# Product steps between the scan's operations: two in a row at every other place

## The chip, the cores and the metric

The kernel runs on one core of a Trainium2 chip. The metric is the device time of one execution in microseconds (us), smaller is better. The core's engines are TensorE (PE in the profile; PEld is its weight load), VectorE (DVE), ScalarE (ACT), GpSimd (POOL) and SyncE (SP), which here only issues DMAs.

## What is computed

The program is a trunk of two layers over 512 latent tokens (and 256 context tokens) of width 1024. Each layer is a token mixer and a mixture of experts:

```
for layer in range(DEPTH):                      # DEPTH = 2
    ...
    bg, cg, ha, rw, ga, gb = split(h_lat @ w_in)            # one wide input product
    ya = (bg * conv(cg * ha)) @ w_a_out                     # branch A: gated convolution
    # branch B: RWKV-7, a scan over tokens, forward and backward, for 8 heads of 64
    s = s * w_t - (s . kk_t) b_t + v_t k_t ;  y_t = s . r_t
    yb = readout(y) @ w_b_out
    y_lat = (sigmoid(ga) * ya + sigmoid(gb) * yb) @ w_o
    ...
    x = x + g2 * hier_moe(h)                                # 32 experts, top 2
```

In layer 0 the context tokens are carried through as well (768 tokens in the products), in layer 1 only the latent ones leave the layer (512 tokens in the products that concern us).

## The kernel before

A layer runs through four stages: `stage_dense` (the columns of `w_in` that the scan needs, and its preparation), `stage_scan`, `stage_out` (`w_b_out`, `w_o`, the router) and `moe` (the experts' weights stream through three rings of buffers, `er`, `ez` and `ex`).

The change is in `stage_scan`. The scan is worked in chunks of 64 tokens, 12 chunks (`NCK`) in each of two passes (`a` = 0, 1, four heads each). The work on a chunk is a chain of small matmuls with copies between them on ACT and DVE:

- `chunk()` prepares the next chunk: transposes L898 (ACT copies L899 and L900), transposes L907 of the keys (ACT copy L909 into `KTr`).
- `step()` is one chunk of the scan: L937 and L941 into `pc`; ACT copies that to `W` (L944); L951 multiplies `W` with the inverse `Rf`; a DVE copy (L952) and an ACT copy (L953) bring the two halves to `VU`; L960 makes the state's update (added on DVE, L964); L975 and L977 make the outputs `Y`.
- `inverses()` makes, for six chunks (`H`) at a time, the triangular inverses `Rf` that those chunks need. It begins with the products L823, then ACT copies L829, a DVE transpose L834, a chain of 31 pairs of DVE operations (L842, L844), two long DVE transposes (L846 into `dgRc`, L848 into `AlTc`), and ends with rounds of L866, ACT copies L870 (`Yb`), L876 and ACT copies L879 on PE and ACT. Each layer makes four such chains; while DVE works at the three later ones, the steps of the six chunks before them run on PE.
- `readout()` normalises the finished outputs: L1000, DVE L1002, ACT L1004, L1008, a row of small DVE operations ending in L304 (`yr`), L1013, and DVE L1015 to L1020.

These chains leave PE idle while a copy runs. So the scan also carries the layer's other products: `fillers()` is a generator over the rest of `w_in` (the convolution's columns, the gates) and the first products of `w_a_out`. One **step** of it (one `next`) is one slice of 128 rows of a product: the three kinds `hh,wh`, `hl,wh` and `hh,wl` of L333, for two column segments in layer 0 (six matmuls) and one in layer 1 (three). Every fourth step begins with the load of a weight tile, which ACT (L314, `wh`) and DVE (L315, `wl`) split into two parts. Before some products stands additional work of the modulation (L653, L252 on PE). The first products of `w_a_out` read `ah` and `al` in place of `hh` and `hl`.

Every `yield w` in `step()`, `chunk()`, `inverses()` and `readout()` is a **place**, where `run()` calls `fill(w)`: it adds `w * FILL[l]` to a debt `owed`, and does a step for each whole unit of it:

```
FILL = (0.75, 0.75)
...
            owed[0] += w * FILL[l]
            while owed[0] >= 1.0:
                owed[0] -= 1.0
                if not held:
                    if next(filler, None):
                        held.append(True)
```

The weights `w` are 1 or 2 in `step()` and `chunk()`, so a place gets none, one or two steps. `held` is set when the products of `w_a_out` reach the point (`HOLD`) from which they are kept for the scan's end.

PE's instructions stand in the order in which the code is written (`tc.manual_schedule` for PE). The orders of DVE, ACT, POOL and SP are made by a scheduler, which has PE's order to go by; they change when the steps move.

Of the kernel before, what the change touches and what calls it, by code (L numbers as in the profile page):

```python
# [116 lines left out]
class Trunk:  # L117
# [606 lines left out]
    def stage_scan(self):  # L724
        nc, tc, t, l = self.nc, self.tc, self.t, self.l
        fp = self.fp
        self.sp = tc.alloc_tile_pool(name=f"sp{l}", bufs=1, side=self.B, reuse_waits="tile")
        self.St = {}
        self.Yt = {}
        filler = self.filler  # L730
        owed = [0.0]
        held = []
        aux = []

        def fill(w):
            if aux:
                aux[0][1] -= 1
                if aux[0][1] < 0:
                    n = next(aux[0][0], None)
                    if n is None:  # L740
                        aux.pop(0)
                    else:
                        aux[0][1] = n
            owed[0] += w * FILL[l]
            while owed[0] >= 1.0:
                owed[0] -= 1.0
                if not held:
                    if next(filler, None):
                        held.append(True)

        def run(gen, pause=False):


            for w in gen:
                if w < 0 and pause:
                    return
                fill(w if w >= 0 else -w - 1)
        with tc.manual_schedule(engines={mybir.EngineType.PE}):
            bs = [(a, g) for a in range(2) for g in range(NCK // H)]
            fill(FIRST[l])  # L760
            inv = self.inverses(*bs[0])
            run(inv)
            cur = self.inv
            nxt = self.chunk(0, 0)
            run(nxt)
            for n, (a, g) in enumerate(bs):
                inv = self.inverses(*bs[n + 1]) if n + 1 < len(bs) else iter(())
                for ii in range(H):
                    i = g * H + ii
                    if ii in RUN[l]:  # L770
                        run(inv, True)
                    mine = self.ch
                    if (n, ii) != (len(bs) - 1, H - 1):
                        nxt = self.chunk(*((a, i + 1) if i + 1 < NCK else (a + 1, 0)))
                    else:
                        nxt = iter(())
                    run(self.step(a, i, *cur, *mine, nxt))
                    for c in SETS:
                        if i == (CCK - 1 if c[1] < CCK else c[1]) and c[0] >= self.c0:
                            aux.append([self.readout(a, c), 0])  # L780
                run(inv)
                cur = self.inv
            held.clear()
            while aux:
                fill(TAIL / FILL[l])
            for _ in filler:
                pass
        self.oa.release()
        self.sp.release()
        fp.release()  # L790
# [784 lines left out]
```

## Time and profile before

| | |
|---|---|
| median of 3 runs | 2934.89 us (2927.92 to 2936.92) |
| the profiled execution | 2937.82 us, span 2935.9 us, mean granted TensorE clock 0.92 |
| PE | 2526.1 us busy, 86% of the span, 17809 matmuls |
| DVE | 1237.9 us, 42% |
| ACT | 837.2 us, 29% |
| POOL | 451.2 us, 15% |
| DMA | mean 251 GB/s |

The share of a whole span is an average over stages with different limits, so the stages are read one by one. The scan of layer 0 lies between about 280 and 824 us of the span, that of layer 1 between about 1793 and 2245 us; the experts of layer 0 run from about 1000 us, those of layer 1 from about 2370 us. The granted clock is given as a share of full speed: 1.00 is 2.4 GHz, 0.50 is 1.2 GHz, a value between is a stretch with some of each. An entry "[0.69 <-ACT KTr L909]" at a row's end is the engine's idle time just before the instruction, and what ended it.

### The profile page before, as it was taken

To read this page: it belongs to the slowest core of one execution; us is meant where nothing else is said; L and a number is where in the kernel's file an instruction comes from. 1 tells how busy PE (TensorE), PEld (TensorE's weight loads), DVE (VectorE), ACT (ScalarE), POOL (GpSimd) and SP (SyncE) were. 2 spreads that over 40 slices of the span, in tenths; PEclk is the share of its full clock that TensorE was granted. 3 is DMA by queue.
4 is the path that set the end of the run, shared out by engine and by line. 5 is a ranking of instruction groups with operands and counts; after the bars stand their busy time and mean duration, and the time that the engine had idled before them with its cause. 6 is when DMAs were issued, how large, how long until landed. Compare 5 with 4: busy or idle time off the path is not lost. (4 is left out here: it accounts for less than half of the span.)

```text
span 2935.9 us, 44964 instructions
## 1 busy us (share of the span) xinstructions
PE 2526.1 (86%) x17809; PEld 1657.8 (56%) x17809; DVE 1237.9 (42%) x2626; ACT 837.2 (29%) x1603; POOL 451.2 (15%) x558
## 2 busy tenths in 40 slices
PE   7898898998889697979796998788988869888896
PEld 5676676777678443434246775566766734333334
DVE  4486654636453411111115686566546421111113
ACT  4453333333222111111112453333442211111111
POOL 0132011111130201111102132011211021111101
PEclk9899999999999798989897999889989979899998
DMA  7657454553553899999984377554445589999993
GB/s 290 211 158 221 169 166 163 180 186 101 173 195 140 324 408 391 391 360 394 383 324 139 110 193 243 180 176 160 153 126 181 221 333 405 408 403 386 400 391 107
DMA packets 287141, 737.21 MB, mean 251 GB/s; under 512 B 57168, under 2 KB 144464, under 8 KB 230864
## 3 DMA queue, kind: packets, MB, share of 16 engines
q1 hardware_dynamic: 273648, 702.83, 66.0%
q0 software_dynamic: 13280, 31.48, 3.3%
q8 instruction: 141, 2.31, 0.3%
q14 instruction: 72, 0.59, 0.1%
HBM read 647.44 MB, written 99.88 MB: 255 GB/s over the span
## 5 line engine op out<-in xcount | busy, mean ns | idle before, releaser
L333 PE MATMUL pd<-hh,wh 128*128 128x512 f32 (+1 forms) x912 | 352.1, 426 | 14.0 <-ACT wh L314 7.9
L333 PE MATMUL pd<-hh,wl 128*128 128x512 f32 (+1 forms) x912 | 311.6, 382 | 11.0 <-DVE wl L315 11.0
L333 PE MATMUL pd<-hl,wh 128*128 128x512 f32 (+1 forms) x912 | 310.6, 381 | 1.3 <-DVE hl L315 1.1
L1413 PE MATMUL pd<-ez,xs 128*64 128x512 f32 x1024 | 255.8, 619 | 42.7 <-DMA ez<-in_w 42.0
L315 DVE TENSOR_TENSOR wl<-wr,wh 128x512 fp32r<-128x512 f32 x236 | 166.0, 704 | 235.4 <-ACT wh L314 234.2
L314 ACT ACTIVATE wh<-wr 128x512 fp32r<-128x512 f32 x236 | 148.5, 630 | 323.1 <-PE pd L333 214.0
L1434 DVE TENSOR_TENSOR yo<-py,yo 64x1024 f32<-64x1024 f32 x65 | 79.0, 1215 | 337.3 <-ACT yo L1433 324.2
L333 PEld LDWEIGHTS pd<-hh,wh 128*128 128x128 f32 x912 | 163.0, 197 | 94.6 <-issue 29.5
L1422 DVE COPY hs<-pd 128x512 f32<-128x512 f32 x65 | 44.9, 690 | 351.1 <-PE pd L1413 312.6
L333 PEld LDWEIGHTS pd<-hh,wl 128*128 128x128 f32 x912 | 163.4, 197 | 47.2 <-DVE wl L315 14.8
L333 PEld LDWEIGHTS pd<-hl,wh 128*128 128x128 f32 x912 | 164.4, 198 | 29.8 <-DVE hl L315 2.6
L1413 PE MATMUL pd<-er,xs 128*64 128x512 f32 x672 | 177.2, 624 | 0.8 <-DMA er<-in_w 0.8
L1413 PEld LDWEIGHTS pd<-ez,xs 128*64 128x64 f32 x1024 | 77.5, 141 | 174.0 <-issue 124.7
L1426 PEld LDWEIGHTS pt<-cst,hs 128*128 128x128 f32 x1040 | 128.7, 197 | 82.1 <-issue 46.2
L1426 PE MATMUL pt<-cst,hs 128*128 128x64 f32 x1040 | 143.3, 287 | 19.0 <-DVE hid L1429 10.7
L1388 POOL DMA_INDIRECT xe<-h2rows,slot x64 | 60.9, 951 | 635.8 <-PE px L1401 616.9
L1413 PE MATMUL pd<-ex,xs 128*64 128x512 f32 x384 | 111.6, 666 | 30.8 <-DMA ex<-in_w 30.8
L1413 PE MATMUL py<-ez,hid 128*64 128x512 f32 x520 | 127.8, 616 | 11.7 <-DVE yo L1434 8.9
L1429 DVE TENSOR_TENSOR hid<-hid,pt 128x256 f32<-128x256 f32 x65 | 27.2, 418 | 234.5 <-ACT hid L1428 233.8
L1424 ACT ACTIVATE hs<-pd 128x512 f32<-128x512 f32 x65 | 38.8, 597 | 288.0 <-PE pd L1413 244.0
L1403 ACT ACTIVATE xs<-px 128x512 f32<-128x512 f32 x65 | 38.7, 597 | 276.7 <-PE pd L1413 142.7
L1433 ACT ACTIVATE yo<-py 64x1024 f32<-64x1024 f32 x65 | 66.4, 1021 | 179.6 <-PE py L1413 152.3
(382 smaller groups left out, 4536.9 us busy)
## 6 DMA issues: line engine op xcount, KB each, us to landing
ez<-in_w SPq DMA_DIRECT2D x193, 1024.0 KB, 16.8
er<-in_w SPq DMA_DIRECT2D x125, 1024.0 KB, 15.4
ex<-in_w SPq DMA_DIRECT2D x72, 1024.0 KB, 13.1
wm<-in_w_mod SPq DMA_DIRECT2D x48, 1024.0 KB, 6.5
wr<-in_w_in SPq DMA_DIRECT2D x172, 256.0 KB, 3.1
bufY<-zrow SPq DMA_DIRECT2D x28, 512.0 KB, 6.8
dKB<-KB SPq DMA_DIRECT2D x16, 768.0 KB, 5.4
dRR<-RR SPq DMA_DIRECT2D x16, 768.0 KB, 4.8
```

Of the source, the lines that this page charges most:

```text
L314: self.nc.scalar.activation(hi, src, AF.Copy)
L315: self.nc.vector.tensor_tensor(lo, src, hi, op=ALU.subtract)
L333: nc.tensor.matmul(p, a[:, k], h[:, kt, s], start=kt == 0 and j == 0, stop=kt == nk - 1 and j == 2)
L1388: self.nc.gpsimd.indirect_dma_start(out=xe[:], out_offset=None, in_=self.h2[:], in_offset=bass.IndirectOffsetOnAxis(ap=slot, axis=0), boun ...
L1403: nc.scalar.activation(xs, ps, AF.Copy)
L1413: nc.tensor.matmul(out[h * CAP:(h + 1) * CAP, c:c + 512], a[:, kt, :], w[:, i + h, c:c + 512], start=kt < 2, stop=kt >= nk - 2)
L1422: nc.vector.tensor_copy(hs, ps)
L1424: nc.scalar.activation(hs, ps, AF.Copy)
L1426: nc.tensor.matmul(pt[:, i, c, :], hs[:, c * P:(c + 1) * P], k["ii"], start=True, stop=True)
L1429: nc.vector.tensor_tensor(hid, hid, pt[:, 1], op=ALU.mult)
L1433: nc.scalar.activation(yo, py[CAP:], AF.Copy)
L1434: nc.vector.tensor_tensor(yo, py[:CAP], yo, op=ALU.add)
```

## The change

The debt is now paid in pairs: `fill()` waits until it is two, and then does two steps at the same place.

```
             owed[0] += w * FILL[l]
-            while owed[0] >= 1.0:
-                owed[0] -= 1.0
-                if not held:
-                    if next(filler, None):
+            while owed[0] >= 2.0:
+                owed[0] -= 2.0
+                for _ in range(2):
+                    if not held and next(filler, None):
                         held.append(True)
```

The steps are the same and as many; PE has as many instructions as before, and its scan operations stand in the same order. What moves are the steps between them. Counted in PE's order, the places that have any step go from 156 to 107 in layer 0 and from 149 to 105 in layer 1, and no place is more than one step ahead or behind of where it was.

On PE, in layer 1, a chunk of the scan after L951 (`pc<-W,Rf`), to the next chunk's transposes. Before:

```order
L951 MATMUL pc<-W,Rf 64x64 x8
L333 MATMUL pd<-hh,wh 128x512
L333 MATMUL pd<-hl,wh 128x512
L333 MATMUL pd<-hh,wl 128x512
L960 MATMUL pc<-VU,KTr 64x64 x8
L333 MATMUL pd<-hh,wh 128x512
L333 MATMUL pd<-hl,wh 128x512
L333 MATMUL pd<-hh,wl 128x512
L898 MATMUL pA<-cst,vfb 128x128 x2
L333 MATMUL pd<-hh,wh 128x512
L333 MATMUL pd<-hl,wh 128x512
L333 MATMUL pd<-hh,wl 128x512
```

The same place on PE after the change:

```order
L951 MATMUL pc<-W,Rf 64x64 x8
L960 MATMUL pc<-VU,KTr 64x64 x8
L333 MATMUL pd<-hh,wh 128x512
L333 MATMUL pd<-hl,wh 128x512
L333 MATMUL pd<-hh,wl 128x512
L333 MATMUL pd<-hh,wh 128x512
L333 MATMUL pd<-hl,wh 128x512
L333 MATMUL pd<-hh,wl 128x512
L898 MATMUL pA<-cst,vfb 128x128 x2
L907 MATMUL py<-cst,KBs 128x128 x4
```

One step each stood before L960, before L898 and before L907; now L960 follows L951 directly, two steps stand before L898, and L907 follows L898 directly.

On DVE, in layer 0, the end of the third of the four inversion chains (the last of its L842 and L844, then the two long transposes), with the `VU` copy L952 of the step that runs beside it. Before:

```order
L842 TENSOR_TENSOR tmp<-AlTc,Tl 128x31
L303 SCALAR_TENSOR_TENSOR yg<-yz,yg 128x4
L844 TENSOR_TENSOR Tl<-Tl,tmp 128x31
L315 TENSOR_TENSOR wl<-wr,wh 128x512
L300 TENSOR_TENSOR yz<-yg 128x4
L846 STREAM_TRANSPOSE dgRc<-Tl 128x32x32
L848 STREAM_TRANSPOSE AlTc<-Tl 128x32x32
L952 COPY VU<-pc 64x256
L301 SCALAR_TENSOR_TENSOR yz<-yz,yv 128x4
```

The same end on DVE after the change:

```order
L842 TENSOR_TENSOR tmp<-AlTc,Tl 128x60
L952 COPY VU<-pc 64x256
L300 TENSOR_TENSOR yz<-yg 128x4
L844 TENSOR_TENSOR Tl<-Tl,tmp 128x2x30
L268 TENSOR_TENSOR mod_83<-pd,pv_82 128x8
L301 SCALAR_TENSOR_TENSOR yz<-yz,yv 128x4
L842 TENSOR_TENSOR tmp<-AlTc,Tl 128x31
L272 SCALAR_TENSOR_TENSOR am_84<-mod_83,pv_82 128x8
L304 SCALAR_TENSOR_TENSOR yr<-yz,yg 128x256
L844 TENSOR_TENSOR Tl<-Tl,tmp 128x31
L846 STREAM_TRANSPOSE dgRc<-Tl 128x32x32
L848 STREAM_TRANSPOSE AlTc<-Tl 128x32x32
```

The `VU` copy and a readout's last operation (`yr`, L304) stood behind the two transposes and now stand ahead of them.

On DVE, in layer 1, the second inversion chain: the place of its last `VU` copy, before:

```order
L842 TENSOR_TENSOR tmp<-AlTc,Tl 128x175
L952 COPY VU<-pc 64x256
L844 TENSOR_TENSOR Tl<-Tl,tmp 128x7x25
L842 TENSOR_TENSOR tmp<-AlTc,Tl 128x156
L844 TENSOR_TENSOR Tl<-Tl,tmp 128x6x26
L842 TENSOR_TENSOR tmp<-AlTc,Tl 128x135
```

That copy after the change:

```order
L842 TENSOR_TENSOR tmp<-AlTc,Tl 128x31
L844 TENSOR_TENSOR Tl<-Tl,tmp 128x31
L846 STREAM_TRANSPOSE dgRc<-Tl 128x32x32
L848 STREAM_TRANSPOSE AlTc<-Tl 128x32x32
L952 COPY VU<-pc 64x256
L315 TENSOR_TENSOR wl<-wr,wh 128x512
L964 TENSOR_TENSOR St_14909<-pc,S_15678 64x4x64 x2
L656 TENSOR_TENSOR mrow<-mrow,pd 128x512
```

It stood seven pairs of the chain ahead of the chain's end; it now stands behind the chain's end and both transposes.

## Rows read from the trace of the kernel before

**Rows 1.** Windows of whole stages: us, busy of each engine, PEclk, DMA share, GB/s.

```profile
280.00:824.00 544.00, 486.57 (x5149) 386.16 (x5150) 291.18 (x743) 183.45 (x419) 73.49 (x126) 0.95 0.51 166
1000.00:1530.00 530.00, 462.23 (x2316) 198.91 (x2314) 78.50 (x120) 80.61 (x126) 55.09 (x60) 0.92 0.98 383
...
1793.00:2245.00 452.00, 378.37 (x4068) 277.84 (x4066) 267.69 (x638) 169.23 (x380) 73.92 (x128) 0.91 0.53 172
```

**Rows 2.** PE's waits, layer 0's scan: us in total, times, longest us.

```profile
PE pA L866 <- DVE AlTc L848: 13.5, 2, 10.7
PE pA L1013 <- DVE yr L304: 12.6, 7, 3.7
PE pd L333 <- ACT ah L314: 6.0, 1, 6.0
PE pc L951 <- ACT W L944: 4.4, 4, 1.6
```

**Rows 3.** PE's waits, layer 1's scan.

```profile
PE pA L866 <- DVE AlTc L848: 22.2, 3, 17.4
PE pA L1013 <- DVE yr L304: 9.7, 6, 4.5
PE pc L960 <- DVE VU L952: 5.1, 8, 2.5
```

**Rows 4.** Timeline of PE, layer 0: start, us, engine line operation xcount.

```profile
381.00 0.62 PE L333 MATMUL pd<-hh,wh 128*128 128x512 f32 x2
...
382.26 0.68 PE L951 MATMUL pc<-W,Rf 64*64 64x64 f32 x16
382.87 0.62 PE L333 MATMUL pd<-hh,wh 128*128 128x512 f32 x2
...
385.18 0.69 PE L960 MATMUL pc<-VU,KTr 128*64 128x64 f32 x16
```

**Rows 5.** Timeline of PE, layer 1, a place with two steps.

```profile
1945.47 0.50 PE L333 MATMUL pd<-hh,wh 128*128 128x512 f32 x1
...
1947.07 0.93 PE L960 MATMUL pc<-VU,KTr 128*64 128x64 f32 x16
```

**Rows 6.** Timelines of ACT, DVE and PE, layer 0: copies that PE waits for.

```profile
351.56 0.99 ACT L870 ACTIVATE Yb<-pA 32x384 f32<-32x384 f32 x2 [1.22 <-PE pA L866]
381.18 0.38 ACT L944 ACTIVATE W<-pc 128x256 f32<-128x256 f32 x1 [1.86 <-PE pc L941]
383.06 0.43 DVE L952 COPY VU<-pc 64x256 f32<-64x256 f32 x1 [3.01 <-PE pc L951]
383.58 0.38 ACT L953 ACTIVATE VU<-pc 64x256 f32<-64x256 f32 x1 [2.02 <-DVE VU L952]
459.19 0.34 PE L975 MATMUL py<-RRs,St 128*64 128x64 f32 x4 [0.69 <-ACT KTr L909]
```

**Rows 7.** Timelines of PE and DVE, layer 0, around the third inversion chain's end.

```profile
693.95 1.20 PE L1013 MATMUL pA<-cst,yr 128*128 128x128 f32 x4 [3.53 <-DVE yr L304]
...
709.87 0.43 DVE L952 COPY VU<-pc 64x256 f32<-64x256 f32 x1
710.35 0.34 PE L960 MATMUL pc<-VU,KTr 128*64 128x64 f32 x4 [1.80 <-DVE VU L952]
711.91 0.57 PE L960 MATMUL pc<-VU,KTr 128*64 128x64 f32 x12 [1.22 <-ACT VU L953]
```

**Rows 8.** Timeline of PE, layer 0, at the second chain's end.

```profile
590.83 1.22 PE L1013 MATMUL pA<-cst,yr 128*128 128x128 f32 x4 [3.65 <-DVE yr L304]
```

**Rows 9.** Timelines of DVE and PE, layer 1, the second chain's end.

```profile
1952.89 2.00 DVE L846 STREAM_TRANSPOSE dgRc<-Tl 128x1024 f32<-128x1024 f32 x1
...
1956.74 0.95 PE L866 MATMUL pA<-AlTc,AM 32*32 32x32 f32 x48 [2.35 <-DVE AlTc L848]
```

**Rows 10.** Windows after waits of PE, layer 0: columns as in Rows 1.

```profile
462.00:480.00 18.00, 14.43 (x232) 11.54 (x232) 4.09 (x3) 7.85 (x13) 2.07 (x3) 0.72 0.30 98
574.00:590.00 16.00, 12.94 (x132) 10.20 (x132) 15.53 (x47) 5.03 (x10) 3.66 (x6) 1.00 0.63 198
```

## The prediction

> **What bounds the kernel now.** I read the windows by stage first [rows 1]. In the experts' stage the DMA share is 0.98: weights stream there, and a change of PE's order before it can only shift when it starts. In the two scans the DMA share is 0.51 and 0.53, and PE is busy 486.57 of 544 us and 378.37 of 452 us. So the scans are bound by PE's own work plus the gaps that PE has to wait out, and the change lies wholly in these two stages. What a scan gains or loses I pass on to the end in full: the stage behind it also runs on PE, and the experts' rings have the same transfers to make whenever they start.
>
> Next come PE's waits in each scan. In layer 0 they are few and long: for the inversion chain's last transpose (L866, 13.5 us in 2 waits), for a readout's `yr` (L1013, 12.6 in 7), for `ah` (6.0 in one), and little for `W` (4.4 in 4) [rows 2]. Layer 1 has the same picture and somewhat more `VU` waits (5.1 in 8) [rows 3]. Two kinds of limit follow. Mostly PE is late by its own work and the steps hide the copies. But while an inversion chain runs, DVE is the late engine, and PE's waits at that chain's end are what is left over: whatever PE loses before them comes out of the wait.
>
> **The price of a step and of a place.** In layer 0 a place with one step takes 1.26 us from its first product to the scan operation behind it (381.00 to 382.26), one with two steps 2.31 (382.87 to 385.18) [rows 4]. So a step is 1.05 us, and each place has about 0.2 us of its own. In layer 1 a place with two steps takes 1.60 [rows 5]; with the same 0.2 a step is 0.70. The change takes the steps from 93 places (49 and 44, from PE's order). If nothing waited at the emptied places it would save 93 x 0.2 = 18.6 us. In fact 29 of the emptied places in layer 0 and 22 in layer 1 hide no copy (before L898, L937, L866 and L907, and behind L1013), and there I take 0.1 to 0.2 each, and nothing between L898 and L907 (9 and 10 of them), two transposes of the same kind: -3.0 us in layer 0, -1.8 in layer 1.
>
> **What the emptied places expose.** The others stand between an operation and the reader of a copy of its result. A place with nothing in it waits for the copy:
> - `KTr` (L907 to L975): the row where it stands bare shows 0.69 us [rows 6].
> - `W` (L941 to L951): the copy is 0.38 [rows 6]; with the latencies on both sides I take 0.55.
> - `VU` (L951 to L960): L952 starts 0.8 us after L951 begins and takes 0.43, L953 follows it for 0.38 [rows 6]; it ends 1.7 us after L951's start, of which L951 itself fills 0.6: 1.1 us.
> - `Yb` (L866 to L876): two ACT copies of 0.99 us together [rows 6]: 1.0.
>
> Against this stands what a one-step place loses anyway (0.1 to 0.2 in layer 0; in layer 1 a step of 0.70 is shorter than the `VU` and `Yb` copies and already leaves up to 0.4). So one emptied place costs, in layer 0, 0.77 (`KTr`), 0.9 (`Yb`), 1.0 (`VU`) and 0.43 (`W`); in layer 1 0.7, 0.65, 0.7 and 0.43. A `W` place right behind products L823 costs the whole step, 1.06 or 0.7, because the copies L829 stand ahead on ACT; the longest such wait before was 1.6 [rows 2]. With the counts from PE's order:
> - Layer 0: 7 `KTr` x 0.77 = 5.4; 3 `Yb` x 0.9 = 2.7; 2 `VU` x 1.0 and one behind L1008 at 0.5 = 2.5; 3 `W` x 0.43 and one behind L823 at 1.06 = 2.4; `W` waits that get a second step -1.7; free places -3.0. Sum +8.3.
> - Layer 1: 2 x 0.7 = 1.4; 4 x 0.65 = 2.6; 5 x 0.7, one at 0.5, and -0.9 for `VU` waits that get a second step = 3.1; `W` 0.43 + 2 x 0.7 - 1.4 = 0.4; free places -1.8. Sum +5.7.
>
> Together +14 us. The lower bound of these terms is the -18.6 from above, with every copy hidden by something else; the upper is +22.8, all positive terms with no saving against them.
>
> **What DVE's new order does.** The scheduler also moves DVE's work, and at the chains' ends this weighs more than any place:
> - Layer 0, third chain. PE waits 3.53 us at L1013 for `yr`, then 1.80 and 1.22 at L960, because the copy L952 stands behind both transposes and starts at 709.87 [rows 7]. In the new order L952 and `yr` stand ahead of them. The three waits are 6.6 us, with a short one nearby 7.0; the chain's own end then becomes the limit, which some of it goes to. Between 0 and -7 I take -5.
> - Layer 0, second chain. L1013 waits 3.65 us for `yr` behind the transposes [rows 8]; `yr` moves ahead of them. L866 will then wait instead, but for less, since L1013 and one step used to stand between: -3.2.
> - Layer 0, first chain: L653's products move ahead of L866's shorter wait (2.8, what is left of 13.5 without the 10.7) [rows 2]: -1.0.
> - Layer 0, `ah`: of the 6.0 us wait [rows 2] the products L937 and L941 now fill 1.1, and a `W` wait of 1.6 behind it gets cover: -2.7.
> - Layer 1, second chain. Here it goes the wrong way: the last `VU` copy moves from seven pairs ahead of the chain's end to behind both transposes, which begin at 1952.89 and end with L866 at 1956.74 after a wait of 2.35 [rows 9]. L960 ran without any wait at 1947.07 [rows 5]; it now waits some 5.6 us, and L866's own 2.35 goes into that, with some 0.4 that the chain ends earlier for having one copy less in it: +2.9.
> - Layer 1, third and fourth chain: waits of L1013 and L866 are long enough [rows 3] to take what the places add: 0.
>
> Layer 0 comes to 8.3 - 1.0 - 3.2 - 5.0 - 2.7 = -3.6; layer 1 to 5.7 + 2.9 - 0.6 (absorbed at the chains' ends) = +8. I make this about **+5 us**. The profiled execution was 2937.8 us, 2.9 above the median of the runs shown (2934.9); on the median the forecast is 2940. A measurement of this kernel can tell about 0.3% (8.8 us) from no change, so this is "within".
>
> **A rule against the sum.** Waiting at more places also touches the granted clock. The rows speak both ways: 462 to 480 us, at whose start PE waits for L866, shows 0.72 with PE busy 14.43 of 18 us; 574 to 590 shows 1.00 with PE busy 12.94 of 16 [rows 10]. The Trainium skill, "TensorE: Matmul & The Clock Gate", section "A second HAM failure mode: psum-queue depth-cycling", says that frequent short idle gaps between groups of matmuls make the clock swing between its levels, and that the throughput is lost there and not in the single matmul. The row of 574 to 590 speaks against it for gaps of this size, the one of 462 to 480 for it; the rival below has its price from rows. In the other direction the Trainium skill, "Perfetto Trace Analysis", section "Matmul Optimizations", asks for matmuls "back-to-back in batches", which is what pairs are; by it the first rival holds.
>
> **Rivals.**
> 1. *The saving at the places prevails* (faster). A copy at an emptied place may be ready sooner than I think. If half of the exposed waits (13.0 in layer 0 and 9.8 in layer 1, all positive terms together) stays hidden, that is -11.4; the third chain gives its whole 7 (-2), and the layer 1 copy is not late for want of PE's readiness (-2.9). 5 - 16.3 = -11, or 2924. For it: more than half of the emptied places hide no copy at all. Against: the bare rows of `KTr` show 0.69 plainly.
> 2. *The clock falls* (slower). The exposed waits put gaps of about 1 us at every second place of the chunks, and the 5.6 us wait of L960 in layer 1 is of the size after which the clock was low before. The stretch 462 to 480 lost at most 18 x (1 - 0.72) = 5 us by it [rows 10]. Three such stretches more make +15: 2955. It decides when waits come in twos or threes within the same chunk.
> 3. *The third chain's gain does not come* (slower). If L952 stands ahead of the transposes in the order but PE's L951 comes so late that DVE waits for it, the chain itself is held up, and the waits go over to L866. Then -5 and -3.2 fall away: 5 + 8.2 = +13, or 2948.
>
> **How the numbers follow.** Forecast 2940: 0.47. Rival 1: 0.16, rival 2: 0.22, rival 3: 0.15. The forecast's own uncertainty is some 9 us to each side (the third chain 0 to -7, the 5.6 us wait, half of the exposed waits), so a bit of it lies beyond either bound. Faster by over 0.3% (under 2926.1): most of rival 1 and little else, 0.16. Slower by over 0.3% (over 2943.7): rivals 2 and 3, less their nearer part, 0.35 in all. Within: 0.49. The range goes from 2922, just below rival 1, to 2957, just above rival 2.
>
> **What would show it.** In the changed profile: PE's waits for `KTr` at L975, for `Yb` at L876 and for `VU` at L960 should rise by about 5 to 7 us each over both scans, and each emptied place of these kinds have 0.55 to 1.1 us. At the third chain of layer 0 the waits of L1013 and L960 should be mostly gone; at the second chain of layer 1 an L960 should wait 4 to 6 us. The scan of layer 0 should be 0 to 7 us shorter, that of layer 1 5 to 11 longer, the rest the same but for its start. A scan with lower clock in many slices shows rival 2; emptied places without waits show rival 1. I would be wrong altogether if another queue decides: weight tiles split late for pairs (`wh`, `wl` waits at L333), or the experts' stage starting in another order.

## The result, and the profile after

The changed kernel takes 2956.78 us (median of 4 runs, 2952.08 to 2959.46) against 2934.88 of the kernel before. The ratio is 1.0076, with a 95% interval from 1.0061 to 1.0091: it is slower by 0.76%, some 22 us. The forecast was 2940 and "within 0.3%"; the time lies just inside the range's upper end, where the second rival (the clock falls, 2955) stood with a chance of 0.22.

The profiled execution took 2958.71 us, its span is 2956.9. Both scans grew: from the first L823 to the first product behind the scan (L1117), layer 0's scan went from 549.2 to 555.3 us, layer 1's from 457.0 to 472.0. These are the windows of exactly these stretches, before (first the stretch and its length, then PE's busy time, PEld, DVE, ACT, POOL, the granted clock, DMA share and GB/s):

```profile
280.50:829.70 549.20, 492.27 (x5166) 390.86 (x5167) 293.99 (x747) 184.12 (x419) 79.19 (x133) 0.95 0.51 167
1793.50:2250.50 457.00, 382.77 (x4079) 281.04 (x4078) 269.70 (x641) 169.74 (x380) 79.24 (x135) 0.91 0.53 173
```

and after the change:

```profile
279.70:835.00 555.30, 491.29 (x5167) 394.02 (x5167) 291.26 (x747) 184.90 (x419) 79.24 (x133) 0.94 0.51 166
1793.20:2265.20 472.00, 388.69 (x4082) 289.52 (x4082) 269.14 (x643) 170.84 (x381) 78.91 (x135) 0.89 0.52 168
```

PE does the same matmuls (the few counts of difference are records that a trace lacks). Its busy time is a little lower in layer 0 and 5.9 us higher in layer 1, with a lower granted clock in both. To split this up I cut each scan into stretches of 4 us, and in each took PE's busy time times (1 - granted clock) as time lost to the clock; what is left of the busy time is work at full clock. It is a reckoning that takes time at 1.2 GHz as half lost. The three add up to the scan's length:

| us | layer 0: length | PE idle | lost to the clock | work at full clock | layer 1: length | idle | clock | work |
|---|---|---|---|---|---|---|---|---|
| before | 549.2 | 56.9 | 21.8 | 470.4 | 457.0 | 74.2 | 28.7 | 354.1 |
| after | 555.3 | 64.0 | 26.0 | 465.3 | 472.0 | 83.3 | 38.8 | 349.9 |
| difference | +6.1 | +7.1 | +4.2 | -5.1 | +15.0 | +9.1 | +10.1 | -4.2 |

So fewer places did save work, 9.3 us, but PE's waits took 16.2 and the clock 14.3. (With stretches of 2 or 8 us the clock's part comes out at 14.6 or 13.4.) The scans grew by 21.1 us and the span by 21.0. That the two agree so well is chance in part: the stages between the scans took 5.6 us less than before, and those behind the second scan 6.3 more.

PE's waits in layer 0's scan after the change (engine, line waited for, us in total, times, longest), to be held against [rows 2]:

```profile
PE pA L866 <- DVE AlTc L848: 15.9, 3, 10.9
PE py L975 <- ACT KTr L909: 12.0, 11, 2.4
...
PE pA L1013 <- DVE yr L304: 4.8, 5, 1.9
PE pc L951 <- ACT W L944: 4.0, 4, 2.5
PE pA L876 <- ACT Yb L870: 2.9, 6, 0.8
PE pc L960 <- DVE VU L952: 2.6, 3, 1.1
PE pd L333 <- ACT ah L314: 2.5, 1, 2.5
```

and in layer 1's, beside [rows 3]:

```profile
PE pA L866 <- DVE AlTc L848: 20.3, 2, 17.4
PE pc L960 <- DVE VU L952: 10.1, 10, 2.3
PE pA L1013 <- DVE yr L304: 8.5, 5, 4.1
...
PE py L975 <- ACT KTr L909: 6.3, 6, 1.6
...
PE pc L951 <- ACT W L944: 5.6, 5, 2.1
PE pA L876 <- ACT Yb L870: 3.8, 9, 0.6
```

Three rows of the kernel before that [rows 2] and [rows 3] don't have, the first from layer 0, the other two from layer 1:

```profile
PE py L975 <- ACT KTr L909: 2.3, 4, 0.7
...
PE py L975 <- ACT KTr L909: 5.1, 8, 1.1
...
PE pA L876 <- ACT Yb L870: 1.1, 2, 1.0
```

In layer 0 the readouts' waits for `yr` fell from 12.6 to 4.8 and that for `ah` from 6.0 to 2.5. In their place came waits for `KTr`: the kernel before has 2.3 us of them in 4 places, now it is 12.0 in 11. In layer 1 it is `VU` that doubled, from 5.1 to 10.1.

**Why `KTr` waits so long.** ACT and PE of the changed kernel, layer 0, at one such place (start, us, engine line operation, and in brackets the idle time before it and what ended it):

```profile
405.17 0.63 ACT L314 ACTIVATE wh<-wr 128x512 fp32r<-128x512 f32 x1 [0.96 <-ACT VU L900]
405.82 0.87 ACT L669 ACTIVATE cg<-pd 128x512 f32<-128x512 f32 x2
406.58 0.60 ACT L909 ACTIVATE KTr<-py 128x512 f32<-128x512 f32 x1
```

```profile
405.27 0.60 PE L907 MATMUL py<-cst,KBs 128*128 128x128 f32 x4
407.24 0.34 PE L975 MATMUL py<-RRs,St 128*64 128x64 f32 x4 [1.37 <-ACT KTr L909]
...
411.54 1.01 PE L333 MATMUL pd<-hh,wh 128*128 128x512 f32 x2
```

PE has done the pair before L907, and the place behind it is bare. The pair ended a product, so ACT has that product's copy (L669) and the next weight tile's split (L314) to do first, and comes to `KTr` late. At other places the two places behind L898 and L907 are both bare, and `KTr`'s copy has to wait for L899 and L900: 0.38 + 0.38 + 0.60 us of ACT in a row, and PE waits 1.04 to 1.10. The prediction had 0.69, from a place where only the last was bare; four of the eleven waits are of that length. The last row shows what came behind it: the first two matmuls of a step take 1.01 us, which took 0.62 in [rows 4].

**The clock.** The same stretch, 404 to 416 us, after the change and before it:

```profile
404.00:416.00 12.00, 10.63 (x78) 7.56 (x78) 1.34 (x4) 2.80 (x6) 2.48 (x5) 0.72 0.51 162
```

```profile
404.00:416.00 12.00, 12.00 (x132) 10.02 (x132) 4.17 (x8) 3.09 (x9) 1.91 (x3) 1.00 0.70 224
```

Behind the wait of 1.37 us PE spent more than half of these 12 us at 1.2 GHz. But the wait alone doesn't decide it. The run `pairs_l0` of the next section has PE's work of layer 0 in the same order as the changed kernel. It has the same wait at the same place (L976 is its L975), and the clock stays at 1.00:

```profile
410.57 0.34 PE L976 MATMUL py<-RRs,St 128*64 128x64 f32 x4 [1.37 <-ACT KTr L910]
```

```profile
407.00:419.00 12.00, 10.63 (x102) 8.42 (x101) 2.93 (x7) 3.65 (x9) 2.82 (x5) 1.00 0.58 179
```

The changed kernel itself waits 1.10 us at an L960 and 1.34 at an L975 between 460 and 467 us, and its row shows the clock at 1.00:

```profile
440.00:470.00 30.00, 26.44 (x278) 20.76 (x277) 29.10 (x97) 8.70 (x21) 4.91 (x9) 1.00 0.45 140
```

The Trainium skill, "TensorE: Matmul & The Clock Gate", section "A second HAM failure mode: psum-queue depth-cycling", tells of a kernel in which frequent short idle times between groups of matmuls make the clock swing. The trace of the changed kernel agrees in the sum (14.3 us more lost, with 16.2 us more idle time); the rows above show that a single wait need not do it.

**The third inversion chain of layer 0**, which had [rows 7]. In order of time it is the fourth, its L846 starting at 705.95 us, and the chain of [rows 8], called the second, is the third; I keep these names. PE after the change:

```profile
700.34 0.68 PE L1013 MATMUL pA<-cst,yr 128*128 128x128 f32 x4 [0.28 <-DVE yr L304]
...
712.45 0.69 PE L960 MATMUL pc<-VU,KTr 128*64 128x64 f32 x16
...
718.84 0.34 PE L975 MATMUL py<-RRs,St 128*64 128x64 f32 x4 [2.37 <-ACT KTr L909]
...
730.93 0.24 PE L876 MATMUL pA<-dgRc,Yb 32*32 32x32 f32 x2 [0.81 <-ACT Yb L870]
```

The waits of 1.80 and 1.22 us at L960 are gone, because L952 now stands ahead of the transposes, and of the 3.53 at L1013 only 0.28 is left. PE is 9.6 us late at the L898 ahead of them and only 0.6 at L866. L898 and L866 before, then after:

```profile
689.60 0.38 PE L898 MATMUL pA<-cst,vfb 128*128 128x128 f32 x2
...
719.65 0.95 PE L866 MATMUL pA<-AlTc,AM 32*32 32x32 f32 x48
```

```profile
699.24 0.38 PE L898 MATMUL pA<-cst,vfb 128*128 128x128 f32 x2
...
720.26 1.49 PE L866 MATMUL pA<-AlTc,AM 32*32 32x32 f32 x48
```

But the 3.53 us did not go by DVE's new order. The `yr` that this L1013 reads was not one behind the transposes: it ran in the middle of the chain, 12.6 us ahead of L846, and it still runs 12.2 us ahead of it (699.77 and 711.96). DVE before, then after:

```profile
693.38 0.42 DVE L304 SCALAR_TENSOR_TENSOR yr<-yz,yg 128x256 f32<-128x256 f32 x1
```

```profile
699.77 0.41 DVE L304 SCALAR_TENSOR_TENSOR yr<-yz,yg 128x256 f32<-128x256 f32 x1
```

It comes 6.4 us later and PE 9.6 us later, so PE's own lateness takes up the wait.

Before L866 PE waits 2.37 us for `KTr` (this chunk's copies stand on ACT behind the inversion's), and in the rounds 0.81 for `Yb`. The windows of the rounds L866 and L876 behind it, after the change and before:

```profile
718.00:738.00 20.00, 17.60 (x292) 14.79 (x294) 1.89 (x4) 7.46 (x17) 1.66 (x3) 0.74 0.26 80
```

```profile
718.00:738.00 20.00, 20.00 (x338) 16.59 (x332) 3.15 (x6) 8.17 (x19) 2.90 (x5) 1.00 0.32 100
```

At the next step's L937 PE is 6.5 us late again (735.80 for 729.33). So 9.0 us of lateness were made up at the chain's end, and 5.9 of them were given back within 16 us. The second chain went the same way: PE is 5.0 us late at the last L907 ahead of it, 2.5 at its first L866, and 7.2 at the L823 behind its rounds.

**The second chain of layer 1**, beside [rows 9]; DVE, then PE:

```profile
1951.06 0.43 DVE L952 COPY VU<-pc 64x256 f32<-64x256 f32 x1
```

```profile
1951.54 0.34 PE L960 MATMUL pc<-VU,KTr 128*64 128x64 f32 x4 [1.15 <-DVE VU L952]
1953.54 0.57 PE L960 MATMUL pc<-VU,KTr 128*64 128x64 f32 x12 [1.66 <-ACT VU L953]
```

The copy stands behind the transposes as its order said, and L960 waits 2.8 us in two parts.

### The profile page after: what moved, and what is told of

Read it like the earlier page. It is cut to its first block, busy times and chain, and to the rows that moved or that the text cites. A ratio compares the mean times of both kernels' runs of the same rounds, so it can differ in the third digit from the quotient of the medians.

```text
span 2956.9 us, 44964 instructions
## 1 busy us (share of the span) xinstructions
PE 2519.9 (85%) x17809; PEld 1666.9 (56%) x17809; DVE 1234.5 (42%) x2626; ACT 838.5 (28%) x1603; POOL 451.5 (15%) x558
## 5 line engine op out<-in xcount | busy, mean ns | idle before, releaser
L333 PE MATMUL pd<-hh,wh 128*128 128x512 f32 (+1 forms) x912 | 345.1, 418 | 15.4 <-ACT wh L314 7.9
L314 ACT ACTIVATE wh<-wr 128x512 fp32r<-128x512 f32 x236 | 148.6, 630 | 359.6 <-PE pd L333 224.8
L333 PEld LDWEIGHTS pd<-hh,wh 128*128 128x128 f32 x912 | 164.0, 197 | 99.7 <-issue 38.6
L1403 ACT ACTIVATE xs<-px 128x512 f32<-128x512 f32 x65 | 38.8, 597 | 289.2 <-PE pd L1413 160.8
L1424 ACT ACTIVATE hs<-pd 128x512 f32<-128x512 f32 x65 | 38.8, 596 | 273.7 <-PE pd L1413 233.9
## 6 DMA issues: line engine op xcount, KB each, us to landing
ex<-in_w SPq DMA_DIRECT2D x72, 1024.0 KB, 14.2
```

The lines of the kernel that those rows point to most:

```text
L314: self.nc.scalar.activation(hi, src, AF.Copy)
L333: nc.tensor.matmul(p, a[:, k], h[:, kt, s], start=kt == 0 and j == 0, stop=kt == nk - 1 and j == 2)
L1403: nc.scalar.activation(xs, ps, AF.Copy)
L1424: nc.scalar.activation(hs, ps, AF.Copy)
```

## The experiments

Executions of one kernel differ by up to 25 us (31 runs of the kernel before: 2922.73 to 2947.32), so I go by the ratio to the runs of the kernel before that were taken beside each experiment.

**One layer at a time.** The pair rule for one layer, single steps for the other:

```
+            n = 2 if l == 0 else 1          # pairs_l0;  pairs_l1: 1 if l == 0 else 2
+            while owed[0] >= n:
+                owed[0] -= n
+                for _ in range(n):
```

> Pairs in layer 0's scan alone, layer 1 as before. In the profile of the changed kernel layer 0's scan was 6.4 us longer, but layer 1's scan began where it began before. Theory (the loss is what layer 1's scan adds, since the experts of layer 0 and the dense stage behind them take the shift up): 2935 to 2939 us. Rival (both scans' losses arrive at the end): 2941 to 2946 us, a third of the whole 21.9.

Measured: 2937.25 us, ratio 1.0020 (1.0002 to 1.0037), in the theory's range.

> Pairs in layer 1's scan alone, layer 0 as before. Theory (the loss comes from layer 1): 2949 to 2957 us. Rival (both scans' losses arrive): 2944 to 2950 us.

Measured: 2945.39 us, ratio 1.0044 (1.0029 to 1.0060), in the rival's range.

Layer 1 has about two thirds of the loss. The two together make 0.64%, near the 0.76% of both. By its interval `pairs_l0` may cost 0.6 to 11 us, so these two runs alone don't settle whether a part of layer 0's loss is absorbed behind its scan. `bare`, below, shows that most of a larger one is not: layer 0's scan ends 34.7 us later there than before (864.4 for 829.7), and layer 1's scan begins 27.8 us later (1821.3 for 1793.5).

Split as above, layer 0 of `pairs_l0` has 65.3 us idle, 21.6 lost to the clock and 465.2 of work, and layer 1 of `pairs_l1` 80.7, 38.6 and 351.9. PE's order in them is that of the changed kernel, and so, nearly, are idle time and work. The clock's loss came back in layer 1 (38.6, where the changed kernel has 38.8 and the kernel before 28.7) and not in layer 0 (21.6, where they have 26.0 and 21.8). The scans with single steps in these two runs lost 22.6 (layer 0) and 30.9 (layer 1). So a loss of about 9 us by the clock in layer 1 is shown twice; that layer 0's 4.2 us come from the change is not shown.

**Pairs only where nothing is copied.** A mark is set at the four kinds of places that hide a copy, and they pay single steps:

```
+            self.copied = True              # ahead of the yields behind L944, L953, L909, L870
             yield 2
...
+            n = 1 if self.copied else 2
+            self.copied = False
+            while owed[0] >= n:
```

> Pairs only at the places that hide no copy: at the four kinds that do (W, VU, KTr, Yb) the debt is paid in single steps, as before. Places with steps: 112 and 110, nearly as few as in the changed kernel (106 and 103); bare copies: W, VU and Yb none, KTr 3 and 3 (changed kernel: 4 and 3, 2 and 5, 3 and 4, 10 and 6). Theory (bare copies and the clock behind them make the loss): the loss goes, 2922 to 2937 us. Rival (two products' steps in a row are bad in themselves, by the split of weight tiles or by DVE's order): 2947 to 2957 us.

Measured: 2930.06 us, ratio 0.9989 (0.9971 to 1.0007). The loss is gone, with nearly as few places as in the changed kernel. Its scans:

```profile
280.20:824.00 543.80, 487.35 (x5166) 388.75 (x5167) 293.23 (x747) 185.13 (x419) 78.77 (x132) 0.94 0.52 168
1783.10:2237.90 454.80, 382.14 (x4081) 283.68 (x4081) 272.10 (x643) 171.64 (x382) 77.78 (x135) 0.91 0.54 175
```

Split as above: idle 56.4 and 72.7, clock 21.2 and 30.2 (both as before), work 466.1 and 351.9: 4.3 and 2.2 us less work. That is what fewer places are worth here, 6.5 us in the profile; on the clock of the whole kernel it can't be told from nothing.

**The converse.** The same mark, with `n = 2 if self.copied else 1`:

> The converse of copies_one: places that hide a copy pay in pairs, so that every second of them is bare (layer 0: W 9, VU 7, KTr 18, Yb 4; layer 1: 10, 8, 11, 5), all other places pay in single steps as before. 118 and 117 places with steps. Theory (bare copies and the clock behind them are the loss, pairs at free places only gain): 40% more W, VU and Yb and 80% more KTr waits than the changed kernel, so 2960 to 2980 us. Rival (pairs as such): 2935 to 2950 us, since most places have one step again.

Measured: 2992.73 us, ratio 1.0198 (1.0175 to 1.0221). More than I expected, though the kernel has more places than the changed one (118 and 117 against 106 and 103; these counts are one or two lower than those of the section on the change). Its waits in layer 0 (L982, L957 and L967 are here what L975, L951 and L960 are before):

```profile
PE py L982 <- ACT KTr L913: 20.5, 18, 4.7
PE pc L957 <- ACT W L949: 12.3, 9, 3.1
```

and its scans took 583.2 and 489.6 us, of which idle 86.1 and 97.9, clock 27.1 and 41.0, work 470.0 and 350.7. With `copies_one` this settles the cause: it is which places are emptied, not that steps stand in pairs. The orders on DVE and ACT differ in these programs too, but the loss follows the bare copies both ways. The clock's share doesn't grow with them: here the scans have 52.9 us more idle time than before and lose 17.6 more to the clock, a third of that, where the changed kernel has 16.2 and 14.3.

**As much cover as can be had.** The places without a copy pay nothing below a debt of four, the others all that is owed:

```
+            n = 4.0 if self.free else 1.0   # set behind L960, L898, L977 and L876
+            self.free = False
+            while owed[0] >= n:
+                owed[0] -= 1.0
```

> The place rule turned round: places that hide no copy (behind L960, L898, L977 and L876) pay nothing until the debt is four, the places with a copy pay all that is owed. 98 and 96 places with steps, no bare copy at all, so up to four steps in a row. Theory: fewer places than the changed kernel and no wait for a copy, so faster than before: 2915 to 2930 us. Rival (steps in a row are bad in themselves): slower than the changed kernel, over 2957 us.

Measured: 2933.01 us, ratio 1.0000 (0.9986 to 1.0014). A miss for the theory as I had put it. Work falls most of all (462.5 and 347.8 us), but idle time rises to 61.2 and 81.8, and the clock's loss to 28.0 and 30.9, though no copy is bare. Why the clock lost 6.2 us more in layer 0 the runs don't show. The idle time rises because PE now comes to the inversion chains' ends too early. In layer 1 (L869 and L1020 are L866 and L1013):

```profile
PE pA L869 <- DVE AlTc L851: 27.6, 3, 17.4
PE pA L1020 <- DVE yr L304: 16.8, 5, 6.0
```

against 22.2 and 9.7 in [rows 3]. What is saved on PE there goes into waits for DVE. The Trainium skill, "Perfetto Trace Analysis", section "Matmul Optimizations", wants matmuls back-to-back in batches; batches of up to four steps brought nothing in this kernel, the ratio is 1.0000.

**Only the costliest wait taken out.** The changed kernel with the mark at L909 alone:

```
             nc.scalar.activation(KTr, ps, AF.Copy)
+            self.copied = True
             yield 1
```

> The changed kernel, but the place behind the transposes of the keys (L907) pays single steps: KTr bare at 2 and 3 places (changed kernel 10 and 6, before 3 and 4), W at 7 and 8, VU at 2 and 2, Yb at 4 and 4. In the changed kernel's trace the KTr waits rose by 10.7 us in layer 0. Theory (KTr is the costliest of the waits, since up to three ACT copies stand in a row there): layer 0's scan comes down by 5 to 8 us, 2944 to 2952 us. Rival (all bare copies cost alike, and the W places that are bare instead take the gain back): 2953 to 2959 us.

Measured: 2956.61 us, ratio 1.0077 (1.0056 to 1.0097): as the changed kernel. `KTr` waits fell from 12.0 to 4.6 us in layer 0, and `W` waits rose from 4.0 to 8.7 there and from 5.6 to 10.8 in layer 1. The rival is right: the debt goes round, and what is not bare at one copy is bare at the next. The clock lost 31.1 and 31.7 us here, 5.1 more than in the changed kernel in layer 0 and 7.1 less in layer 1, so the number of bare copies alone doesn't set that loss.

**Work under the bare waits.** Dummy matmuls where a place had no step, into a PSUM tile from which nothing reads their results:

```
+        ps = self.psum("pc", [P, 2, P], 2)      # allocated ahead of the yield
         yield 2
-        ps = self.psum("pc", [P, 2, P], 2)
+        self.warm(ps[:, 0, :], 4)               # if not self.paid: n matmuls ident x ident
```

> The changed kernel, with dummy matmuls (128 columns, results overwritten) on PE at the W, VU, KTr and Yb places that have no step: 4, 8, 6 and 8 of them, 152 in layer 0 and 180 in layer 1. They are extra work under the wait for the copy. In the changed kernel's scans the clock cost 4.2 and 10.1 us more than before, PE's idle time 7.1 and 9.1 more. Theory (the bare waits lower the clock and that is half of the loss): the clock's loss falls back to about 22 and 29 us, 2944 to 2950 us. Rival (the clock falls for other reasons, and the waits are the whole loss): the clock's loss stays near 26 and 39 us, 2955 to 2962 us.

Measured: 2944.02 us, ratio 1.0030 (1.0015 to 1.0046). It is 0.46% faster than the changed kernel although PE does 34.0 and 41.6 us more work. Its scans:

```profile
279.00:835.80 556.80, 513.56 (x5471) 419.96 (x5471) 293.71 (x747) 184.96 (x419) 78.78 (x132) 0.96 0.51 165
1790.00:2257.50 467.50, 407.85 (x4441) 316.55 (x4441) 269.87 (x644) 171.98 (x382) 79.82 (x135) 0.94 0.53 171
```

Idle 43.2 and 59.7, clock 14.2 and 16.3: less lost to the clock than even in the kernel before. So with work under the bare waits less is lost to the clock, as it should be if the waits lower it. But the dummies do more than undo the change, as the clock's loss is smaller than in the kernel before, and the scheduler also made another order on DVE for this program, which this run doesn't separate.

> The run warm with about half the dummy matmuls: 2 at a bare W place, 4 at VU, KTr and Yb (90 and 102 in all). In warm each took some 0.23 us (work at full clock rose by 34.0 us for 152 and 41.6 for 180), longer together than the waits they stood under; now they are about as long as the waits. Theory (work under a bare wait keeps the clock, and costs nothing if it is no longer than the wait): 20 and 23 us more work, idle time down by about 16 and 18, the clock's loss near that of warm (14 and 16): 2932 to 2940 us, level with before. Rival (the clock needs as much work as in warm): clock loss back at 24 and 35, 2950 to 2958 us.

Measured: 2951.86 us, ratio 1.0061 (1.0046 to 1.0076), in the rival's range. In layer 0 it went as the theory has it (length 551.4 for 555.3, clock 16.9 for 26.0); in layer 1 the clock lost 32.1, and the scan took 476.2, longer than without the dummies. With 102 dummies in place of 180 only 6.7 of the 22.5 us by which `warm` lowered the clock's loss are left there.

**Work under the waits at the chains' ends**, on top of `copies_one`; `ps` is the tile that L866 writes next (`copies_warm` also has 4 dummies in each `Yb` place of layer 1):

```
+            if j == 0 and (a or gi):
+                self.warm(ps, 20)               # copies_warm8: 8
```

> copies_one with dummy matmuls on PE ahead of the first L866 of the three later inversion chains of each layer (20 each, under a wait of some 2.4 us) and, in layer 1, 4 in each Yb place. In the kernel before, layer 1's clock is at half from 1957 to 1974 and 2150 to 2170 us, right behind such a wait. Theory (a short wait lowers the clock for the rounds behind it, and work under the wait prevents it): the clock's loss in layer 1 falls from 30 to under 22 us, 2918 to 2926 us. Rival (the clock follows something else): as copies_one or up to 5 us slower, 2928 to 2937 us.

Measured: 2942.12 us, ratio 1.0030 (1.0018 to 1.0042). Too much: the clock lost 14.8 and 25.7, but the work rose by 14.0 and 20.7.

> copies_one with 8 dummy matmuls (1.8 us) ahead of the first L866 of the three later chains of each layer, where copies_one waits 1.7 to 2.7 us, and none in the rounds (copies_warm had 20 and 4: 13.9 and 20.7 us more work than copies_one, for 6.4 and 4.5 less lost by the clock). Theory: 5.5 us more work in each scan under waits of that size, the clock's loss down by 5 in each: 2918 to 2926 us. Rival (the dummies lie beyond the waits in some chains): no better than copies_one, 2928 to 2936 us.

Measured: 2920.93 us, ratio **0.9957** (0.9943 to 0.9971). This is the fastest, ahead of both kernels. Its scans:

```profile
279.90:822.20 542.30, 486.66 (x5215) 389.95 (x5215) 293.37 (x747) 185.03 (x419) 78.65 (x132) 0.96 0.53 170
1775.10:2233.50 458.40, 389.09 (x4130) 291.40 (x4130) 269.68 (x643) 171.60 (x382) 80.02 (x135) 0.90 0.54 174
```

In layer 0 the clock lost 13.7 us (21.2 in `copies_one`). In layer 1 it lost 32.0, no less than without (30.2), where the theory had 5 us less.

> The kernel before, with single steps everywhere, and the same 8 dummy matmuls ahead of the first L866 of the later chains as in copies_warm8. It splits that run's 13 us. Theory (about half of it is the clock behind the chains' ends, half the fewer places of copies_one): 2925 to 2931 us. Rival (the dummies alone make it): 2919 to 2924 us. Rival (the places alone): 2931 to 2937 us.

Measured: 2936.74 us, ratio 1.0016 (1.0003 to 1.0030). By its time this is the third (the places alone), at the upper edge; but the places alone are `copies_one`, with 0.9989. So none of the three holds: the dummies alone do slight harm to the kernel before (clock 19.5 and 37.2, work 476.2 and 357.8), and the gain of `copies_warm8` is that of neither part alone.

> copies_warm8 with 2 dummy matmuls in each Yb place of layer 1, where a step of 0.70 us is shorter than the two copies of 0.99, so that PE idles in each round; 16 in all, 3.7 us of work. In copies_warm8 the clock is still at half from 1944 to 1956 us, in the rounds behind the second chain. Theory: the clock's loss in layer 1 falls from 32 by 4 to 8 us, 2914 to 2920 us. Rival (the short idle times of 0.2 to 0.3 us don't matter): 2921 to 2926 us.

Measured: 2925.20 us, ratio 0.9979 (0.9967 to 0.9991). The clock lost 27.6 in layer 1 (32.0) but 19.2 in layer 0, where nothing was changed (13.7). It is faster than the kernel before, by 0.1 to 0.3%, and its ratio is above that of `copies_warm8`, so this run shows no gain from dummies under the short waits of 0.2 to 0.3 us. I can say that `copies_warm8` beats the kernel before by 0.3 to 0.6%, but not from which wait each part comes: the clock's loss in a scan moves by 4 to 6 us between programs that differ elsewhere.

## Why the prediction was wrong, point by point

- **Which stage, and what bounds it**: right. The change is in the scans, and their growth is the growth of the span. That a shift is passed on was right in the main: in the changed kernel the stages outside the scans moved by -0.8, -5.6 and +6.3 us, and in `bare` 27.8 of 34.7 us reached layer 1.
- **The price of a place**: 0.2 us each, an upper end of 18.6, of which I counted 4.8 at places without a copy. The work at full clock fell by 9.3 (changed kernel) and 6.5 (`copies_one`). Right in kind, and half of it in size: 9.3 us over 93 places is 0.1 each, where 0.2 had been read at one place.
- **Waits at emptied places**: `Yb` right (2.7 and 2.6 expected, 2.9 and 2.7 measured: from none to 2.9, from 1.1 to 3.8). `W` about right. `VU` in layer 1 with the copy behind the transposes: 3.1 + 5.6 expected, +6.0 measured; the 5.6 us wait was 2.8, as the chain's end itself came 6 us earlier on DVE (1947.10 for 1952.89). **`KTr` mis-sized**: 5.4 us in layer 0, and it was 10.7 (2.3 to 12.0, and 1.0 at an L977). The row it rested on [rows 6] has ACT idle when L907 ends; the order showed that L898's place is emptied as often, and I gave that place a price of nothing because its two neighbours are transposes, without asking what it gives ACT time for.
- **DVE's new order at the chains' ends**: right for the two waits of L960 at the third chain, 3.0 us, and for the second chain, where PE made up 2.5 us (3.2 forecast). The 3.53 us of the third chain were misread: that `yr` never stood behind the transposes, and its wait went because PE came late. That `yr` waits fell by 7.8 in all, more than the 3.53 and 3.65, is therefore luck in part. The first chain's L866 waits 2.62 for 2.83, where 1.0 less was forecast; `ah` is down by 3.5, less 1.4 at `al` (2.7 forecast).
- **The clock: the step that failed.** Without it the scans would have grown by 1.9 and 4.9 us, together 6.8 where I had said 5. The sum had no term for it; in the trace of the changed kernel it was worth 14.3 us. Of this the 10.1 in layer 1 came again in `pairs_l1`, and the 4.2 in layer 0 did not come again in `pairs_l0`. The rows spoke both ways [rows 10], and I left it to a rival. I had also misread one of them: the row of 574 to 590 us, which was to speak against the clock, ends before the 3.65 us wait does (590.83 [rows 8]), and behind that wait the kernel before shows the clock near half:

```profile
590.80:594.00 3.20, 3.17 (x21) 2.63 (x23) 1.56 (x5) 0.49 (x1) 1.04 (x1) 0.55 0.44 154
```

The sum itself put 30 new waits of 0.5 to 1.1 us into the scans (16 and 14), and a part of them should have had a price for the clock. The runs give no fixed one: the clock's loss rose by nearly nothing (layer 0 of `pairs_l0`) to nine tenths (the changed kernel) of what the idle time rose by. And a gain at a chain's end is worth less than the wait that goes, because the rounds behind it have bare `Yb` copies, and there the clock was lower after the change (0.74 for 1.00 at 718 to 738 us).
- **Luck**: that the rest came to 6.8, so near 5. By layer I had -3.6 and +8, and without the clock it was +1.9 and +4.9. In layer 0 `KTr` was too low by 5.3 us and the 3.53 us were not a gain of the order; in layer 1 the `VU` term was too high by 2.7; and fewer places saved more work than the 4.8 us counted.
- **The rivals**: the second came nearest. The clock fell, by 14.3 us where it had 15 (three stretches of 5 us). That its 2955 is so near the measured time is luck in part: the 5.6 us wait that it named was 2.8, and the sum that it stands on had layer 0's scan shorter by 3.6, where it grew by 1.9 without the clock. The first (waits hidden) fell with the wait rows. The third fell too: the waits of L960 went, and what PE made up was given back behind the chain.

## What to carry to other kernels

Filler work between a chain's small operations has two jobs, and its place matters more than its grouping: where the next operation reads a copy, the place must not be bare, and the other places can be emptied. When a change empties places, count for each what the copying engine still has queued at that moment, and allow for each new wait on PE to cost a second time, in the clock behind it: here between nothing and nine tenths of the idle time. Group the fillers where nothing waits, and look at which engine sets the end of each stretch first: what PE saves while DVE is the late engine comes back as waiting.

## What the runs showed of the hardware that I had not expected

Short waits on PE cost clock, but at no fixed rate. The scans of the changed kernel had 16.2 us more idle time than before and lost 14.3 us more to the clock; those of `bare` 52.9 and 17.6; layer 0 of `pairs_l0` 8.4 and nothing. The same wait of 1.37 us, with PE's work in the same order, was followed by a granted clock of 0.72 over 12 us in the changed kernel and of 1.00 in `pairs_l0`. Useless matmuls under these waits made the changed kernel faster by 0.46% (`warm`, ratio 1.0030 for 1.0076), though they were 75.6 us of extra work on the engine that bounds the scans; a dummy matmul of 128 columns in f32 took some 0.23 us. With 192 in place of 332 of them, less was still lost to the clock in layer 0 (16.9 us for the changed kernel's 26.0), and most of the effect was gone in layer 1 (32.1 for 38.8, where `warm` had 16.3).
